# A two-layer trunk on one core: projection weights cast one unit ahead, squares a block later, and a one-product scale

## The chip, the cores and the metric

The kernel runs on one core of a Trainium2 chip. The metric is the device time of one execution in microseconds (us), as the median of several runs. The engines are TensorE (PE: matmuls, with PEld for its weight loads), VectorE (DVE), ScalarE (ACT), GpSimd (POOL) and SyncE (SP, which here issues nearly all DMA transfers). Each engine works through its own instructions in order, and semaphores tie the engines together.

## The reference

A trunk of two pre-norm residual layers over 1024 positions of width 1024, all in float32, and a last norm. The first mixer is a recurrent layer (LRU) of width 1536, the second is attention with 16 heads of 64 and a forget gate (FoX). Cut to what matters:

```python
def lru_mixer(h, ...):
    u = h @ w_in                                   # 1024 -> 2 * 1536
    xb, gate = u[..., :1536], u[..., 1536:]
    xc = causal_depthwise_conv(xb, conv_w, conv_b)
    r, i = sigmoid(block_diag(xc, wa, ba)), sigmoid(block_diag(xc, wx, bx))
    log_a = -8 * r * softplus(-a_param)
    hs = scan(exp(log_a), sqrt(-expm1(2 * log_a)) * i * xc)
    return (hs * silu(gate)) @ w_out

def fox_mixer(h, ...):
    u = h @ w_in                                   # q, k, v, gate, and 16 columns of forget logits
    cum = cumsum(log_sigmoid(f_logit + b_f))
    logits = q @ k.T / 8 + cum[query] - cum[key], masked to key <= query
    return (softmax(logits) @ v * silu(gate)) @ w_out

x = x + lru_mixer(rms_norm(x, g0)); x = x + fox_mixer(rms_norm(x, g1)); out = rms_norm(x, gf)
```

## The kernel before

All work is in one function, `trunk`, written as Python generators that a tile scheduler orders further. Products keep float32 accuracy by splitting each operand into a high and a low part. A product is then three matmuls (high by high, high by low, low by high), and each weight needs two casts: the high part by ACT, and the low part by DVE or POOL.

Four stages follow one another. From about 20 to 440 us run twelve LRU blocks (`for n in range(NB)`). Each loads its weights, casts them (`wh` by ACT, `wl` by POOL or DVE), projects (`ups`, `gps`), and runs convolution, gates and scan on DVE and ACT. Beside this, `some()` lets ACT square a piece of the attention weights (`wsf`), whose norms set the scale with which those weights become float16.

From 440 to about 517 us runs the passage between the layers: the last output products (`ops`), the squares of the new x (`squares`), and then `input_scale(h)` for each half of the sequence. There `xnorm` sums eight columns of squares over all partitions, ACT takes the root (`unit_x`), and DVE forms `gx`, the scale with which `split_input` makes the float16 parts of the layer's input (`h16`). `sscol` are the column sums for the norm itself. The first value products (`vps`) and the first projections of keys and queries (`gps1`) follow.

From 517 to 950 us come the attention heads. A head's work is a string such as `"1.1..1.1..00"`. `run` walks through it: a digit takes a step of the head's own work (1 for scores and maxima, 0 for the weighted sum) and a dot takes one step of the `fill`, which is projection work for later heads, so that PE always has something to do. Scores S go into two PSUM buffers. Each is masked by DVE with its maximum `m`, turned into `p` by an exponential on ACT, normalised to `pp` (ACT the high, DVE the low part), transposed by a DMA (`pT`), and used for O. In heads 3, 7 and 11 the values of the next four heads are projected (`values(g)`, products `vps`).

Projection weights of attention are loaded into raw tiles (`wf`, three buffers) and cast by `split16` into float16 tiles (`w16`, `w` in the profile). `weights16` and `values` call it, and load and casts stand in one place of the program. The scheduler is free to lift them as far as buffers and dependences allow. `tc.issue_after` ties an instruction behind a given one.

From 950 us on come the output projection and the last norm.

The raw tiles come from here:

```python
    return wpool.tile([P, *shape], F32, tag="wf", name="wf", bufs=3)
```

The functions that the change touches:

Of the kernel before, what the change touches and what calls it, by code (L numbers as in the profile page):

```python
# [40 lines left out]
def trunk(ctx: ExitStack, tc: tile.TileContext, xt, w0, wg, wo0, pc, gn, gf, w1, wv, wf, bf, wo1, out):  # L41
# [157 lines left out]
    with ExitStack() as l0:  # L199
# [378 lines left out]
        for h, cs in enumerate(halves):  # L578
# [45 lines left out]
    with ExitStack() as l1:  # L624
# [10 lines left out]
        def fixed_rows():  # L635
            for s in range(2):
                nc.gpsimd.memset(f32(T[s][64:, 1]), 1.0)
                for u in U[s][s:]:
                    nc.vector.memset(f32(u[64:, 1]), 0.0)
                    nc.vector.memset(f32(u[64:68, 1]), -1.0)  # L640

        slots = itertools.cycle(("wh", "wl"))

        def split16(src, shape, b):
# [4 lines left out]
            both = wpool.tile([P, 2, *shape], FP16, tag=next(slots), name="w16")  # L649
# [3 lines left out]
            return [(hi[:, k], lo[:, k]) for k in range(shape[0])]  # L653

        def weights16(b):

            for k in range(0, KT, 4):
                yield from split16([(w1[b][:, k : k + 4], slice(0, P))], (4, P), 4 + b)

        def project(b, w, use, hs=(0, 1)):  # L660

            for h in hs:
                pt = ps.tile([P, HALF], F32, tag="g", name="gps1")
                yield from gemm_steps(pt, zip(w, hT[h]))
                nc.vector.scalar_tensor_tensor(pt, pt, unit_w[:, 4 + b : 5 + b], rs1[h], ALU.mult, ALU.mult)
                use(h, pt)

        def values(g):

            ex = HEADS if g == 0 else 0  # L670
            parts = []
            for k in range(0, KT, 2):
# [12 lines left out]
            for st, k in todo:  # L685
# [18 lines left out]
                for a in range(2):  # L704
                    v = vpool.tile([P, 4, HD], FP16, tag=f"v{st}", name=f"v{st}", bufs=2)
                    src = pt[:, a * P : (a + 1) * P].rearrange("p (b d) -> p b d", b=2)
                    rv_ = rv[:, g, st : st + 1]
                    to_hi(v[:, 0::3], src, nc.scalar, scale=rv_)
                    nc.vector.scalar_tensor_tensor(v[:, 1:3], src, rv_, v[:, 0::3], ALU.mult, ALU.subtract)
                    Vs[2 * g + a].append(v)  # L710
                if ex:
                    nc.vector.tensor_scalar(fz[:, st], pt[:, 256:], rf[:, st : st + 1], None, ALU.mult)
# [10 lines left out]
        def kq_units(pair, parts=((1, (0, 1)), (0, (0, 1)))):  # L723

            for is_k, hs in parts:
                if is_k not in kq:
                    kq[is_k] = tuple(
                        kqpool.tile([P, SEQ], F32R, tag=f"qk{p}{is_k}", name=f"qk{p}") for p in "hl"
                    )
                if hs[0] == 0 or pair == 0 or is_k and pair in (3, 5, 7):  # L730
                    kqw[is_k] = list(weights16(is_k * 8 + pair))
                hi, lo = kq[is_k]

                def use(h, pt):
                    eng = nc.scalar if pair or h else nc.vector
                    cs = halves[h]
                    if is_k:
                        to_hi(hi[:, cs], pt, eng)
                        to_lo(lo[:, cs], pt, hi[:, cs], nc.vector)
                    else:  # L740
                        to_hi(hi[:, cs], pt, eng, scale=0.125)
                        nc.vector.scalar_tensor_tensor(lo[:, cs], pt, 0.125, f32(hi[:, cs]), ALU.mult, ALU.subtract)  # L742

                yield from project(is_k * 8 + pair, kqw[is_k], use, hs)
# [47 lines left out]
        drain(kq_units(0, ((1, (0,)), (0, (0,)))))  # L792
# [53 lines left out]
        def g_units(pair, hs=(0, 1)):  # L846

            if hs[0] == 0:
                sgs[pair] = at.tile([P, SEQ], F32, tag="sg", name="sg1")
                gw[0] = list(weights16(16 + pair))  # L850
            sg = sgs[pair]

            def use(h, pt):
                g_ = sg[:, h * HALF : (h + 1) * HALF]
# [3 lines left out]
            yield from project(16 + pair, gw[0], use, hs)  # L858
# [97 lines left out]
        seen = [None]  # L956

        behind = []

        def run(order, *gens, fill=iter(()), side=iter(()), vals=None):  # L960

            for n, i in enumerate(order):
                if vals and n == order.rfind("1"):
# [185 lines left out]
        fill = kq_units(0, ((1, (1,)), (0, (1,))))  # L1149
# [6 lines left out]
        fill = g_units(0)  # L1156
# [7 lines left out]
        for hd in range(HEADS):  # L1164
            pair = hd // 2
            if hd % 2 == 0:
                if hd < 12:
                    fill = kq_units(pair + 1, ((1, (1,)), (0, (0, 1))))
                    if hd == 0:
                        fill = chain(kq_units(1, ((1, (0,)),)), fill)  # L1170
                elif hd == 12:
# [4 lines left out]
                        kq_units(7, ((1, (1,)), (0, (0, 1)))),  # L1176
                        g_units(7, (0,)),
                        high_y(0),
                        first_out(),
                        beside(g_units(7, (1,)), 1, splits[0]),  # L1180
# [6 lines left out]
            elif pair < 6:  # L1187
                fill = chain(g_units(pair + 1), kq_units(pair + 2, ((1, (0,)),)))
# [4 lines left out]
            run(first, weigh(hd, 0), maxima(hd, 1), fill=fill, side=side)  # L1193
# [10 lines left out]
            vals = None  # L1204
            if hd % 4 == 3 and hd < 12:
                vals = values(hd // 4 + 1)
# [92 lines left out]
```

## Time and profile before

| What | us |
|---|---|
| Median of 3 runs | 1077.0 (1075.47 to 1083.69) |
| Profiled execution | 1077.86 |
| Its span | 1076.1 |
| PE busy | 1036.2 (96% of the span) |
| DVE busy | 789.2 |
| ACT busy | 657.7 |
| POOL busy | 108.8 |
| Mean granted clock of PE | 0.989 |

The span is the time from the first to the last instruction of the profiled execution. PE is the busiest engine by far, and what it waits for is shown in the views of its waits and in the timelines. Lines of a view begin with the start, or with the engine and the line of the program; a bracket at the end gives the idle time before an instruction and what released it. Several groups share one line because helpers issue them: L57 is every ACT instruction of the helper, L69 every matmul, and L66 every load.

### The profile page before, as it was taken

The page shows a single profiled execution, that of the slowest core. Times are in us where ns is not written, and L with a number is a line of the kernel's source. Part 1 is how long each engine was busy: PE and PEld are TensorE (multiplying, and loading weights), DVE is VectorE, ACT ScalarE, POOL GpSimd, SP SyncE. Part 2 cuts the span into 40 slices and gives each one's busy share as a digit, 9 for nine tenths or more (in the row PEclk, how much of TensorE's full clock was granted, in tenths as well). Part 3 has the DMA queues.
Part 4 walks back from the last instruction along what each step waited for, and adds up shares of the span by engine and source line. Part 5 has one row for each costly group of instructions (what it writes and reads, how often), then busy time and mean ns, then how long its engine had stood idle before and what let it go on. Part 6 is the DMA issues. An engine that isn't in the chain of part 4 may idle for free. (4 is left out here: it accounts for less than half of the span.)

```text
span 1076.1 us, 15162 instructions
## 1 busy us (share of the span) xinstructions
PE 1036.2 (96%) x5130; PEld 728.0 (68%) x5130; DVE 789.2 (73%) x1463; ACT 657.7 (61%) x1199; POOL 108.8 (10%) x87
## 2 busy tenths in 40 slices
PE   8998999999999999999899999999999999999997
PEld 6786788788888888766445566544755447577676
DVE  7788686657756868897778876878578884886675
ACT  8468756565657475565666655656466664754454
POOL 1312122022212220001000000000000000012110
PEclk9998999999999999999999999999999999999999
DMA  7112433233323311443678994888848895689984
GB/s 246 60 44 84 118 113 103 84 99 113 102 74 98 122 57 50 148 149 87 164 154 169 180 192 116 154 178 173 177 115 180 168 187 125 129 175 236 257 200 157
DMA packets 219805, 148.92 MB, mean 138 GB/s; under 512 B 161936, under 2 KB 174864, under 8 KB 219728
## 3 DMA queue, kind: packets, MB, share of 16 engines
q1 hardware_dynamic: 217328, 140.09, 54.0%
q0 software_dynamic: 2400, 7.87, 2.4%
q8 instruction: 40, 0.66, 0.3%
q14 instruction: 37, 0.30, 0.1%
HBM read 73.33 MB, written 11.67 MB: 79 GB/s over the span
## 5 line engine op out<-in xcount | busy, mean ns | idle before, releaser
L69 PE MATMUL gps<-h,w 128*128 128x512 f16 x1152 | 272.6, 384 | 2.3 <-DVE qkl L742 2.3
L69 PEld LDWEIGHTS <-w 128*128 128x128 f16 x1152 | 104.8, 99 | 130.2 <-issue 19.8
L57 ACT ACTIVATE p<-S,m 128x128 f32<-128x128 f32 (+7 forms) x128 | 94.2, 736 | 61.8 <-DVE m L889 37.5
L69 PE MATMUL S<-T,U 96*128 96x512 f32 (+7 forms) x384 | 106.3, 386 | 17.9 <-ACT p L57 17.8
L110 POOL TENSOR_TENSOR wl<-wf,wh 128x512 fp32r<-128x512 f32 x46 | 87.5, 1910 | 315.8 <-ACT wh L57 203.1
L57 ACT ACTIVATE pp<-p,sums 128x128 f16<-128x128 f32 (+7 forms) x128 | 95.5, 770 | 33.2 <-DVE sums L901 12.4
L903 DVE SCALAR_TENSOR_TENSOR pp<-p,sums,pp 128x128 f16<-128x128 f32 (+7 forms) x128 | 102.8, 813 | 13.1 <-ACT pp L57 12.2
L889 DVE CUSTOM_DVE_ANT_0 S<-S,mask 128x128 f32<-128x128 f32 (+7 forms) x128 | 97.1, 759 | 11.1 <-PE S L69 10.1
L69 PEld LDWEIGHTS S<-T,U 128*128 128x128 f32 (+1 forms) x384 | 67.2, 190 | 43.6 <-ACT p L57 29.5
L69 PE MATMUL vps<-w,h 128*128 128x256 f16 (+1 forms) x768 | 88.4, 277 | 0.5 <-ACT v L57 0.5
L57 ACT CAST wh<-wf 128x512 fp32r<-128x512 f32 x88 | 51.5, 592 | 56.6 <-PE ops L69 31.2
L69 PEld LDWEIGHTS <-h 128*128 128x128 f16 x768 | 75.8, 99 | 12.2 <-ACT v L57 0.8
L69 PE MATMUL gps<-hh,wl 128*128 128x512 f32 x192 | 76.8, 400 | 4.6 <-POOL wl L110 4.5
L69 PE MATMUL ops<-yh,wh 128*128 128x512 f32 x192 | 77.4, 403 | 0.7 <-DVE x L403 0.7
L69 PE MATMUL ups<-hh,wh 128*128 128x512 f32 x192 | 76.2, 398 | 1.4 <-ACT hh L57 1.3
L69 PE MATMUL ops<-yh,wl 128*128 128x512 f32 x192 | 76.3, 397 | 0.7 <-DVE wl L110 0.7
L69 PE MATMUL ups<-hl,wh 128*128 128x512 f32 x192 | 76.3, 397 | 0.2
L69 PE MATMUL ups<-hh,wl 128*128 128x512 f32 x192 | 75.7, 394 | 0.8 <-POOL wl L110 0.8
L69 PE MATMUL gps<-hl,wh 128*128 128x512 f32 x192 | 76.4, 398 | 0.0
L69 PE MATMUL gps<-hh,wh 128*128 128x512 f32 x192 | 76.4, 398 | 0.0
L69 PE MATMUL ops<-yl,wh 128*128 128x512 f32 x192 | 75.6, 400 | 0.0
L57 ACT ACTIVATE w<-wf,wsq 128x512 f16<-128x512 f32 (+1 forms) x74 | 52.4, 717 | 37.8 <-PE gps L69 14.2
(197 smaller groups left out, 1910.7 us busy)
## 6 DMA issues: line engine op xcount, KB each, us to landing
wf<-in_w SPq DMA_DIRECT2D x106, 256.0 KB
wsf<-in_w SPq DMA_DIRECT2D x48, 256.0 KB
wf<-in_wo SPq DMA_DIRECT2D x64, 128.0 KB
T<-qkh SPq DMA_DIRECT2D x64, 128.0 KB
U<-qkh SPq DMA_DIRECT2D x64, 128.0 KB
x<-in_xt SPq DMA_DIRECT2D x16, 256.0 KB
wsf<-in_wv SPq DMA_DIRECT2D x16, 256.0 KB
x1d<-x SPq DMA_DIRECT2D x16, 256.0 KB
```

The source lines that it names most:

```text
L57: act[0] = op(*args, **kw)
L69: pe[0] = nc.tensor.matmul(*args, **kw)
L110: return eng.tensor_tensor(lo, src, f32(hi), ALU.subtract)
L889: nc.vector.tensor_tensor_reduce(S[:, :n], S[:, :n], mask[:, SEQ - n :], -1.0, -NEG, ALU.add, ALU.min, accum_out=m)
L903: nc.vector.scalar_tensor_tensor(both[:, :, 1], p, r, both[:, :, 0], ALU.mult, ALU.subtract)
```

## The change

Five things are changed.

The squares of the attention weights begin in block 3 of the LRU and no longer in block 2; `some()` is called once more in each block.

In the passage, `xnorm` is one product of eight columns for each half. ACT copies its result into `gx` and sums the eight columns on the way (`accum_out`), and takes the root from that sum. The last square of the first half is added up like the others by DVE, without the flag `wait`.

The rows of U that hold constants are written by ACT copies of `onesf` with a scale of 0 or -1, not by DVE memsets.

Weights of projections are objects (`Weights`) with a load and a cast of their own. `play` walks through the units of a plan. In the last half of a unit it loads the next unit's weights at step 0, and casts them at step 2, tied behind `seen[0]`, which is the last exponential. All fills are planned ahead in the list `fills`.

`values` loads its first two weights in the first run of the head (`soon`), and casts them before the second run; the last two are loaded and cast in the second run.

```diff
         def some():
-            if n > 1:
+            if n > 2:
                 with tc.issue_after(act[0].ins):
                     next(wsquares, None)
...
             product(ups[1], 1, wu)
+            some()
...
             nc.vector.tensor_tensor(xsq[h], xsq[h], g2, ALU.mult)
-            all_ = ps.tile([P, 1], F32, tag="O", name="xnorm")
-            for k in range(KT):
-                matmul(all_, onesf, xsq[h][:, k : k + 1], start=k == 0, stop=k == KT - 1)
-            nc.scalar.activation(unit_x[h], all_, AF.Sqrt, bias=tiny, scale=1.0 / TOP / TOP)
+            all_ = ps.tile([P, KT], F32, tag="O", name="xnorm")
+            matmul(all_, onesf, xsq[h], start=True, stop=True)
+            nc.scalar.activation(gx[h], all_, AF.Copy, accum_out=unit_x[h])
+            nc.scalar.activation(unit_x[h], unit_x[h], AF.Sqrt, bias=tiny, scale=1.0 / TOP / TOP)
...
-                        wait=h == 0 and db == KT - 1,
                         accum=xsq[h][:, db : db + 1],
...
                 for u in U[s][s:]:
-                    nc.vector.memset(f32(u[64:, 1]), 0.0)
-                    nc.vector.memset(f32(u[64:68, 1]), -1.0)
+                    for rows, value in ((slice(64, P), 0.0), (slice(64, 68), -1.0)):
+                        one = onesf[rows, :1]
+                        nc.scalar.activation(
+                            u[rows, 1], one.to_broadcast([one.shape[0], HALF]), AF.Copy, scale=value
+                        )
...
+        class Weights:
+            def load(self):
+                if self.raw is None:
+                    self.raw = [
+                        load16([(w1[self.b][:, k : k + 4], slice(0, P))], (4, P), 4 + self.b) for k in range(0, KT, 4)
+                    ]
+            def cast(self):
+                self.load()
+                if self.parts is None:
+                    self.parts = [x for r in self.raw for x in cast16(*r)]
+                return self.parts
...
+        def play(units):
+            for u in units:
+                u["start"]()
+                w, h = u["w"], u["h"]
+                after_ = [v["w"] for v in plan[plan.index(u) + 1 :] if v["w"] is not w][:1]
                 pt = ps.tile([P, HALF], F32, tag="g", name="gps1")
+                for i, _ in enumerate(gemm_steps(pt, zip(w.cast(), hT[h]))):
+                    if h == u["last"] and seen[0] is not None:
+                        for v in after_:
+                            if i == 0:
+                                v.load()
+                            elif i == 2:
+                                with tc.issue_after(seen[0].ins):
+                                    v.cast()
+                    yield
...
         def values(g):
-            parts = []
+            parts, raw = [], []
             for k in range(0, KT, 2):
...
-                parts += split16(src, (2, 256 + ex), g)
-                if k == 2 or k == 6 and not ex:
+                raw.append(load16(src, (2, 256 + ex), g))
+                if k == 2 and not ex:
+                    yield
+                if k % 4 == 0:
+                    continue
+                with tc.issue_after(seen[0].ins) if k == 2 and not ex else nullcontext():
+                    parts += [x for r in raw for x in cast16(*r)]
+                raw = []
+                if k == 2 or not ex:
                     yield
...
             for n, i in enumerate(order):
+                if soon and n == order.rfind("1") + 1:
+                    next(soon)
                 if vals and n == order.rfind("1"):
                     next(vals)
```

How this moves instructions stands at three places. The first is ACT in head 3, from the end of one run of scores into the next. `w16` from `wf_5389` is the second value weight; `wf_5401` and `wf_5403`, and in the rows of before `wf_5854` and `wf_5940`, are weights of projection units. Before:

```order
L57 ACTIVATE yo_5160<-O_5418,wsq_238 64x512
L57 ACTIVATE p_5447,sums_5440<-S_5442,m_5445 128x128
L57 ACTIVATE w16_5856<-wf_5854,wsq_238 128x512
L57 ACTIVATE p_5468,sums_5440<-S_5463,m_5466 128x256
L57 ACTIVATE sg1_5313<-gps1_5405 128x512
L57 ACTIVATE w16_5942<-wf_5940,wsq_238 128x512
```

And with the change:

```order
L57 ACTIVATE yo_5145<-O_5411,wsq_238 64x512
L57 ACTIVATE w16_5426<-wf_5389,wsq_238 128x512
L57 ACTIVATE p_5436,sums_5429<-S_5431,m_5434 128x128
L57 ACTIVATE w16_5450<-wf_5401,wsq_238 128x512
L57 ACTIVATE w16_5453<-wf_5403,wsq_238 128x512
L57 ACTIVATE p_5463,sums_5429<-S_5458,m_5461 128x256
L57 ACTIVATE sg1_5308<-gps1_5394 128x512
```

The cast that stood behind the first exponential (128x128) now stands ahead of it, and two more casts stand ahead of the second one.

The second place is SP in the same head, with the change: the transfers around the last value load, `wf_5510`.

```order
L66 DMA wf_5502<-in_w1 128x512
L66 DMA wf_5504<-in_w1 128x512
L66 DMA wf_5508<-in_wv 128x512
L967 DMA_TRANSPOSE pT_5430<-pp_5438 128x2x128
L967 DMA_TRANSPOSE pT_5430<-pp_5465 128x4x128
L66 DMA T1_3806<-cumd_3798 2x512
L967 DMA_TRANSPOSE pT_5430<-pp_5486 128x6x128
L66 DMA T1_3806<-qkh_3822 64x512
L66 DMA wf_5510<-in_wv 128x512
```

Three raw loads go out together and fill the three buffers. The fourth comes six transfers later, when the cast of `wf_5508` has given its buffer back.

The third place is ACT in the LRU around block 2, where `wh` is the weight whose low part POOL makes. Before:

```order
L57 CAST xch_629<-xc_623 128x1024
L57 ACTIVATE wsf_596,vsq_237<-wsf_596 128x256 x2
L57 ACTIVATE ti_570<-gate_586,hbx_111 128x512
L57 CAST yh_591<-a_522 128x1024
L57 ACT_TABLE_LOAD
L57 ACTIVATE m2_719<-m2_719 128x1024
L57 CAST wh_900<-wf_898 128x512
```

And with the change:

```order
L57 CAST xch_627<-xc_621 128x1024
L57 ACTIVATE ti_570<-gate_586,hbx_111 128x512
L57 CAST yh_591<-a_522 128x1024
L57 ACT_TABLE_LOAD
L57 ACTIVATE m2_703<-m2_703 128x1024
L57 CAST wh_876<-wf_874 128x512
```

The pair of squares `wsf_596` ahead of the cast `wh` is gone from this block. The order of PE is the same in both kernels from the first scores of attention to the end.

More of the change, by code (lines that the diff above doesn't have):

```diff
@@ L848, in g_units, with start @@
             if hs[0] == 0:
-                sgs[pair] = at.tile([P, SEQ], F32, tag="sg", name="sg1")
-                gw[0] = list(weights16(16 + pair))
-            sg = sgs[pair]
+                gw[0] = Weights(16 + pair)
+            def start():
+                if pair not in sgs:
+                    sgs[pair] = at.tile([P, SEQ], F32, tag="sg", name="sg1")
             def use(h, pt):
-                g_ = sg[:, h * HALF : (h + 1) * HALF]
+                g_ = sgs[pair][:, h * HALF : (h + 1) * HALF]
                 nc.scalar.activation(g_, pt, AF.Tanh, scale=0.5)
                 nc.vector.scalar_tensor_tensor(g_, g_, 1.0, pt, ALU.add, ALU.mult)
-            yield from project(16 + pair, gw[0], use, hs)
+            units = [job(gw[0], h, start, use) for h in hs]
+            for u in units:
+                u["last"] = hs[-1]
+            return units
         stats, pT = {}, {}
@@ L1148, in late @@
                 late_w.append((wh, wl))
-        fill = kq_units(0, ((1, (1,)), (0, (1,))))
+        fills = [kq_units(0, ((1, (1,)), (0, (1,)))), g_units(0), []]
+        for pair in range(7):
+            if pair == 0:
+                fills[-1] += kq_units(1, ((1, (0,)),))
+            fills[-1] += kq_units(pair + 1, ((1, (1,)), (0, (0, 1))))
+            if pair < 6:
+                fills += [g_units(pair + 1) + kq_units(pair + 2, ((1, (0,)),)), []]
+        last_g = [g_units(7, (h,)) for h in range(2)]
+        fills = iter(fills)
+        fill = play(next(fills))
         gates1 = forget(1)
@@ L1155, in trunk @@
         drain(fill)
-        fill = g_units(0)
+        fill = play(next(fills))
         for _ in range(4):
@@ L1167, in trunk @@
                 if hd < 12:
-                    fill = kq_units(pair + 1, ((1, (1,)), (0, (0, 1))))
-                    if hd == 0:
-                        fill = chain(kq_units(1, ((1, (0,)),)), fill)
+                    fill = play(next(fills))
                 elif hd == 12:
@@ L1187, in trunk @@
             elif pair < 6:
-                fill = chain(g_units(pair + 1), kq_units(pair + 2, ((1, (0,)),)))
+                fill = play(next(fills))
             first, second = LAST if hd > 11 else ORDER
@@ L1192, in trunk @@
             side = chain(pieces(hd + 1, 0, 0), pieces(hd + 1, 0, 1)) if hd else iter(())
-            run(first, weigh(hd, 0), maxima(hd, 1), fill=fill, side=side)
+            vals = values(hd // 4 + 1) if hd % 4 == 3 and hd < 12 else None
+            run(first, weigh(hd, 0), maxima(hd, 1), fill=fill, side=side, soon=vals)
             drain(side)
@@ L1203, in trunk @@
                 side = chain(side, late())
-            vals = None
-            if hd % 4 == 3 and hd < 12:
-                vals = values(hd // 4 + 1)
+            if vals:
                 next(vals)
```

88 lines of the change are left out of this document (50 added, 38 removed).

## The prediction

> **What bounds the kernel now.** I read four views in this order: the engines' busy time, the list of what TensorE (PE) waits for, the timelines around its longest waits, and the granted clock by stretch.
>
> ```profile
> PE 1036.2 (96%) x5130; PEld 728.0 (68%) x5130; DVE 789.2 (73%) x1463; ACT 657.7 (61%) x1199; POOL 108.8 (10%) x87
> PE S L69 <- ACT p L57: 17.8, 19, 2.0
> PE gps L69 <- POOL wl L110: 4.5, 1, 4.5
> PE gps L69 <- DVE qkl L742: 2.3, 1, 2.3
> ```
>
> The first row is each engine's busy time, the others are PE's waits: total, count, longest. PE is busy for 1036.2 of the span's 1076.1 us, so about 40 us are to be had from waits. The rest must come from fewer matmul passes or from a better clock. Of the waits, 17.8 us stand before score products (S), whose PSUM buffer is freed by an exponential (p) on ScalarE (ACT). The timeline names what holds the exponential back:
>
> ```profile
> 659.47 0.72 ACT L57 ACTIVATE w<-wf,wsq 128x512 f16<-128x512 f32 x1 [1.84 <-DMA wf<-in_w]
> 660.10 0.78 ACT L57 ACTIVATE p<-S,m 128x640 f32<-128x640 f32 x1
> 661.01 0.98 PE L69 MATMUL S<-T,U 128*128 128x512 f32 x4 [2.02 <-ACT p L57]
> 702.67 0.74 PE L69 MATMUL S<-T,U 128*128 128x512 f32 x2 [2.00 <-ACT p L57]
> 788.50 1.01 PE L69 MATMUL S<-T,U 128*128 128x512 f32 x4 [2.03 <-ACT p L57]
> ```
>
> The columns are start, duration, engine and operation, with the idle time before it in brackets. At 659.47 a weight cast waits 1.84 us for its own DMA. The exponential behind it starts at 660.10, and PE goes on at 661.01 after 2.02 us.
>
> ```profile
> 88.00:100.00 12.00, 7.54 (x22) 5.67 (x22) 10.90 (x9) 11.16 (x25) 5.68 (x1) 0.72 0.37 117
> 440.00:460.00 20.00, 19.21 (x93) 14.91 (x92) 16.73 (x31) 12.59 (x29) 0.00 (x0) 0.91 0.43 147
> 470.00:490.00 20.00, 20.00 (x140) 14.59 (x137) 18.54 (x40) 12.02 (x24) 2.18 (x3) 0.91 0.39 119
> 655.00:665.00 10.00, 7.99 (x49) 5.17 (x47) 7.29 (x18) 6.94 (x14) 0.00 (x0) 1.00 0.33 107
> 784.00:794.00 10.00, 7.97 (x34) 4.10 (x32) 6.89 (x17) 6.21 (x12) 0.00 (x0) 0.83 0.46 134
> ```
>
> These rows give a stretch, its length, the busy time of PE, PEld, DVE, ACT and POOL, the granted clock, the DMA share and GB/s. The loss to the clock is length times (1 - clock): 12 x 0.28 = 3.4, twice 20 x 0.09 = 1.8, nothing, and 10 x 0.17 = 1.7 us. The first and last of these stand around waits of 4.46 and 2.03 us. At 440 and 470 PE hardly idles; around the wait of 661.01 the clock is whole.
>
> By the Trainium skill (TensorE: Matmul & The Clock Gate, Part 1: The HAM clock gate) the clock falls to half after an idle window of about 3.4 us. The rows for 440, 470 and 784 disagree: the clock fell there with no wait over 2.03 us. By that rule alone the change would not win the clock terms below, and the sum would be 3.5 us higher.
>
> **Part 1, the scale product in the passage.** Two groups of one-column products stand in the path of PE:
>
> ```profile
> 450.87 1.84 PE L69 MATMUL xnorm<-xsq,onesf 128*128 128x1 f32 x16
> 452.57 1.93 PE L69 MATMUL sscol<-onesf,sq 128*128 128x1 f32 x16
> 475.76 1.92 PE L69 MATMUL xnorm<-xsq,onesf 128*128 128x1 f32 x16
> 477.54 1.03 PE L69 MATMUL sscol<-onesf,sq 128*128 128x1 f32 x8
> ```
>
> Sixteen passes fill 450.87 to 452.57, or 1.70 us. Over all four rows 56 passes take 6.2 us, 0.11 each. The change makes each xnorm one product of eight columns (two passes each), which removes 28 passes. Summing the last square of the first half on VectorE (DVE) removes 8 more sscol passes. That is 36 x 0.11 = **-4.0 us**. The eight-column product is not in the trace; I price it like a one-column pass. Both low-clock stretches of the passage begin right behind these rows. With 1.1 us of such passes in place of 3.5 and 2.7 the clock may hold: **-2.5**, between 0 and -3.6. Against this, the first half's scale now stands behind an added copy with a sum and behind squares of the second half on ACT, and PE takes up the first projection earlier. A wait of 0 to 3 us can appear: **+1**.
>
> **Part 2, squares a block later.** The LRU's longest wait, under the row of its group (busy time, then the mean of one in ns):
>
> ```profile
> L110 POOL TENSOR_TENSOR wl<-wf,wh 128x512 fp32r<-128x512 f32 x46 | 87.5, 1910 | 315.8 <-ACT wh L57 203.1
> 83.13 0.43 ACT L57 ACTIVATE wsf<-wsf 128x256 f32<-128x256 f32 x1
> 83.85 0.20 ACT L57 ACTIVATION_READ_ACCUMULATOR wsf<-wsf 128x1 f32 x1
> 86.86 1.22 DVE L311 TENSOR_TENSOR us<-ups,rs 128x1024 f32<-128x1024 f32 x1
> 87.84 1.13 ACT L57 CAST wh<-wf 128x512 fp32r<-128x512 f32 x2
> 88.00 1.21 DVE L110 TENSOR_TENSOR yl<-a,yh 128x1024 fp32r<-128x1024 f32 x1
> 88.52 5.68 POOL L110 TENSOR_TENSOR wl<-wf,wh 128x512 fp32r<-128x512 f32 x1 [14.64 <-ACT wh L57]
> 94.26 0.79 PE L69 MATMUL gps<-hh,wl 128*128 128x512 f32 x1 [4.46 <-POOL wl L110]
> ```
>
> The POOL subtraction takes 5.68 us beside a run of DVE operations, and PE waits 4.46 for it. The change removes the squares that stood ahead of the cast wh: some 0.8 us from 83.13 on. It also puts yl ahead of us on DVE, so that POOL's operation meets a DVE operation that reads PSUM. If POOL then takes 1.9 us, the mean of its group, the wait and its 3.4 us of clock go, together -7.9. If only the start moves, -0.8. The later blocks get the squares instead, which could cost 1. I take **-3.5**, a little under half of the best case.
>
> **Part 3, start of attention.** Late casts there end in waits of PE:
>
> ```profile
> 488.33 1.57 DVE L639 MEMSET U<- 64x512 f32 x3 [0.16 <-DVE v L709]
> 507.13 0.72 ACT L57 ACTIVATE w<-wf,wsq 128x512 f16<-128x512 f32 x1 [2.30 <-DMA wf<-in_w]
> 509.33 1.33 ACT L57 ACTIVATE w<-wf,wsq 128x512 f16<-128x512 f32 x2 [1.22 <-DMA wf<-in_w]
> 521.05 1.46 PE L69 MATMUL gps<-h,w 128*128 128x512 f16 x6 [2.32 <-DVE qkl L742]
> 523.75 0.62 PE L69 MATMUL S<-T,U 128*128 128x384 f32 x2 [1.24 <-ACT p L57]
> ```
>
> The change loads these weights a unit earlier, so 3.5 us of ACT waits leave the chain to qkl. Of PE's 2.32 + 1.24 I take **-2.5**, between 0 and -3.6. U's constants move from DVE (three of the six memsets take 1.57 us) to six ACT copies, some 0.7 us each if they run like the casts above. The vps products of that place cover both, so they cost nothing, and up to 1 us if a v eviction slips.
>
> **Part 4, weights one unit ahead.** The weights cast at 659 and 786 are now loaded some 20 us before their use by the order of the units, so the waits of 2.02 and 2.03 go, with perhaps half of the 1.7 us of clock at 786: **-5**, between 0 and -5.8. The wait at 702.67 stays, since the order there is as before. Moving casts off DVE near 600, 727 and 853 should save about 0.7 each, the 0.74 us of the DVE cast at 594.39 below: **-2**, between 0 and -2. Two or three unit weights keep only 2.3 to 3.7 us between issue and use, where the two loads in the rows below take 2.8 and 3.8 from issue to the cast's start: **+1.5**, between 0 and +3.
>
> Against this stand the **values stages** (heads 3, 7 and 11). Before, their weights were cast during earlier heads. Now all four casts, and four unit casts, come within about 20 us. The same place in the trace, with the two rows just used on top:
>
> ```profile
> 594.39 0.74 DVE L652 SCALAR_TENSOR_TENSOR w<-wf,wsq,w 128x512 f16<-128x512 f32 x1
> 656.70 1.25 SPq L66 DMA_DIRECT2D wf<-in_w  x2
> 623.62 1.55 SPq L66 DMA_DIRECT2D wf<-in_w  x3
> 625.40 0.37 ACT L57 ACTIVATE p<-S,m 128x128 f32<-128x128 f32 x1
> 627.46 0.72 ACT L57 ACTIVATE w<-wf,wsq 128x512 f16<-128x512 f32 x1 [1.60 <-DMA wf<-in_w]
> 625.91 0.62 PE L69 MATMUL S<-T,U 128*128 128x384 f32 x2 [0.19 <-ACT p L57]
> 628.69 0.73 PE L69 MATMUL S<-T,U 128*128 128x512 f32 x2 [0.84 <-ACT p L57]
> 635.97 9.22 PE L69 MATMUL vps<-w,h 128*128 128x256 f16 x83
> 635.67 1.24 ACT L57 ACTIVATE pp<-p,sums 128x384 f16<-128x384 f32 x2
> ```
>
> First wait: the load issued at 623.62 lands at 627.46, after 3.8 us. Before, the exponential at 625.40 stood ahead of its cast. Now a value cast stands ahead of that exponential. It can start only at 627.46 + 0.63 = 628.1, and with two more casts of 0.72 before the second exponential the next S slips from 628.69 to about 631.5: **+2.8**. If the load lands as the cast comes up, 0.
>
> Second wait: raw weights have three buffers, and the last value load now waits for the cast before last. That cast follows the two normalisations (pp) that end at 636.91 in the last row, later by up to the 2.8 just found; its two halves take 1.4, so it ends between 638.3 and 641.1, say 639.8. A load of 2.8 to 3.8 us and the last cast's own 1.4 make the last weight ready at 644.0 to 645.0. PE, at 0.11 us per vps, needs it 30 products into the stage: 635.97 + 2.8 + 3.3 = 642.1. That is a wait of 1.9 to 2.9; the other ends of the cast give 0.4 and 4.2. I take **+1.9**, since SP has less queued there. Behind these casts on ACT stand the evictions v, and behind those the value products' PSUM.
>
> Together 4.7 in each of three stages, **+14**; between 0 and 3 x (2.8 + 4.2 + 1.7) = 26, the last term for a drop of the clock as at 784.
>
> By the Trainium skill (DMA: Bandwidth & Descriptors, two cost components) a transfer costs about 2.0 us plus its bytes at 436 GB/s, which for these 256 KB is 2.6 us. The row at 623.62 shows 3.8, with other transfers in flight. With the page's 2.6 the first wait would be 1.2 us shorter and the second 0.2, and the sum by it some 4 us lower, towards the faster case below.
>
> **The sum.** -4.0 - 2.5 + 1 - 3.5 - 2.5 - 5 - 2 + 1.5 + 14 = -3.0 us. The profiled execution took 1077.86 us (span 1076.1 and 1.8 around it), 0.9 above the median of 1077.0. So 1077.86 - 3.0 = **1074.9 us**.
>
> **The rivals.**
>
> *Faster, 1062 us.* The loads land before their casts come up in the values stages. For it: SP then has fewer issues ahead of them, and the load at 656.70 took 2.8 us. Against it: the third-buffer chain is fixed by the allocation. The stages then cost 1 us each, not 4.7 (-11), and part 2 wins 2 more: 1074.9 - 13 = 1062.
>
> *Slower, 1090 us.* In each values stage the waits come at 2.8 and 2.9 us and the clock falls behind them, as behind 2.03 us at 784: 7.4 each, 22 in all, +8 against my sum. The wait in the passage takes its 3 (+2), and parts 2 and 3 and the passage's clock win only 3 of 8.5 (+5.5): 1074.9 + 15.5 = 1090. For it speaks that the first wait is tied to one load's place; against it, that at 659 a wait of 2.02 us left the clock whole. It decides from about 6.8 us per stage: the other terms are -17 as I take them and -9.5 if these fail, and 1% is 10.8.
>
> *It does little, 1078 us.* PE's order from the first S on is the one of before, and each wait may only move to the next exponential. Then the passage's 4 us stay and the stages take them back. This lies within the same 1% as my forecast.
>
> **How the numbers follow.** I give my forecast 0.28 and doing little 0.14, together 0.42 within 1% (1066 to 1088); 1% is about what a measurement of this kernel can tell from no change. The faster case has 0.34, since most terms are gains read from single waits and only one term is a large loss. The slower case has 0.24. With all gains whole and no loss the sum is about -27 us (1051), and with all losses and only the 4.0 of the passage won +30 (1108). The range for 8 in 10 leaves a tenth at either end: 1056 to 1092. The forecast's own range is 1066 to 1082.
>
> **What would show it.** Right: PE's wait on POOL wl falls below 2 us, xnorm shows 4 passes, and no S waits 2 us in the places of 659 and 786. Right for the loss: in heads 3, 7 and 11 a value cast on ACT waits for its DMA with an exponential behind it, and PE's vps wait on DVE w or ACT w, about 4 us per stage. Wrong: vps runs without a break in these stages (then it is the faster case), or the clock's low stretches become more than before (the slower one).

## The result and the profile after

The changed kernel takes 1086.2 us (median of 14 runs, 1083.6 to 1092.4), the kernel before 1077.5 in its runs beside it. The ratio is 1.0073 with a 95% interval of 1.0053 to 1.0093: **slower by 0.7%**, where the forecast was 1074.9. The profiled execution took 1086.31 us with a span of 1084.5.

PE's waits in the changed kernel (total, count, longest):

```profile
PE S L69 <- ACT p L57: 11.9, 6, 4.2
PE gps L69 <- DVE w L661: 9.8, 8, 2.0
PE vps L69 <- ACT v L57: 7.8, 1, 7.8
PE gps L69 <- ACT w L57: 1.9, 1, 1.9
```

The wait on POOL's wl of 4.5 us and the one on qkl of 2.3 are gone, and the waits before S fell from 17.8 us in 19 to 11.9 in 6. But the longest of them are now over 4 us, and two kinds are new: 11.7 us of projections (gps) that wait for a weight cast (w), and 7.8 us of value products (vps) that wait for an eviction.

Where the time went is seen from the first exponential of the heads, before and after:

```profile
523.24 0.36 ACT L57 ACTIVATE p<-S,m 128x128 f32<-128x128 f32 x1
```

```profile
514.33 0.36 ACT L57 ACTIVATE p<-S,m 128x128 f32<-128x128 f32 x1
```

The first exponential comes 8.9 us earlier, and the last matmul ends 8.4 us later. Of the 8.9 us, 5.3 are there at the first score product (512.65 against 517.91); the rest are the waits of 2.32 and 1.24 us at the start of attention, which are gone. So the stages up to here win 8.9 us in these two executions, and attention from here on loses 17.3.

**What won.** In LRU block 2, POOL's subtraction and the DVE operation beside it (after), and the clock there:

```profile
87.36 1.51 POOL L110 TENSOR_TENSOR wl<-wf,wh 128x512 fp32r<-128x512 f32 x1 [13.85 <-ACT wh L57]
87.63 1.21 DVE L311 TENSOR_TENSOR us<-ups,rs 128x1024 f32<-128x1024 f32 x1
88.00:100.00 12.00, 11.45 (x51) 9.01 (x49) 11.78 (x11) 10.28 (x15) 0.86 (x1) 1.00 0.25 71
```

POOL's subtraction starts 1.16 us earlier, lies for most of its time beside the operation that reads PSUM, and takes 1.51 us where it took 5.68. PE does not wait, and the granted clock of the stretch is 1.00 where it was 0.72. In the passage xnorm is down to four passes (count, then minimum, median and maximum in ns), and the low clock around it is gone:

```profile
L69 PE MATMUL xnorm<-xsq,onesf x4: 170/214/256, 444.3 to 466.4; 128*128 128x8 f32 x4
440.00:460.00 20.00, 19.96 (x93) 13.15 (x93) 19.13 (x40) 16.28 (x39) 0.00 (x0) 1.00 0.55 175
```

**What lost.** First, still ahead of attention, a new wait at the passage's end:

```profile
470.98 5.00 ACT L57 ACTIVATE h<-x,gx 128x512 f16<-128x512 f32 x8
478.32 1.66 ACT L57 ACTIVATE U<-onesf 64x512 fp32r<-64x512 f32 x3 [1.88 <-DVE h L573]
480.01 0.88 ACT L57 ACTIVATE v<-vps,rv 128x128 f16<-128x128 f32 x3
484.01 1.52 PE L69 MATMUL vps<-w,h 128*128 128x272 f16 x6 [7.83 <-ACT v L57]
476.00:488.00 12.00, 4.17 (x26) 2.86 (x25) 5.97 (x17) 7.81 (x17) 4.28 (x5) 0.72 0.44 99
```

PE began the value products 16 us earlier than before. It ran through what PSUM holds, and then waited for evictions that stand on ACT behind the second half's split (h) and U's copies. The granted clock of this stretch is 0.72.

Second, a unit weight whose cast is tied behind an exponential, in head 5:

```profile
664.79 1.01 SPq L66 DMA_DIRECT2D wf<-in_w  x2
697.23 0.37 ACT L57 ACTIVATE p<-S,m 128x128 f32<-128x128 f32 x1
697.59 0.71 ACT L57 ACTIVATE w<-wf,wsq 128x512 f16<-128x512 f32 x1
699.99 0.74 DVE L661 SCALAR_TENSOR_TENSOR w<-wf,wsq,w 128x512 f16<-128x512 f32 x1
700.79 1.43 PE L69 MATMUL gps<-h,w 128*128 128x512 f16 x5 [2.03 <-DVE w L661]
```

The second of the two loads at 664.79 (matched by the order of instructions) brings the weight that is cast at 697.59, some 32 us later and right behind the exponential. PE needs it at 698.4 and waits 2.03 us, until its low part, which DVE takes up at 699.99 behind other work, is done. Four more places show the same.

Third, the value stage of head 3:

```profile
617.89 0.59 SPq L66 DMA_DIRECT2D wf<-in_wv  x1
622.29 0.72 ACT L57 ACTIVATE w<-wf,wsq 128x512 f16<-128x512 f32 x1 [2.63 <-DMA wf<-in_wv]
622.92 0.35 ACT L57 ACTIVATE p<-S,m 128x128 f32<-128x128 f32 x1
623.41 1.01 PE L69 MATMUL S<-T,U 128*128 128x384 f32 x2 [3.40 <-ACT p L57]
```

The load takes 4.4 us to the cast, the exponential waits behind the cast, and PE waits 3.40. In heads 7 and 11 the same wait is 2.75 and 4.19 us. The clock falls behind these waits and behind some of those for unit weights:

```profile
520.00:530.00 10.00, 7.68 (x30) 4.00 (x30) 6.79 (x18) 7.74 (x14) 0.00 (x0) 0.83 0.79 170
620.00:632.00 12.00, 7.73 (x24) 3.31 (x24) 8.43 (x23) 6.08 (x16) 0.00 (x0) 0.72 0.91 218
698.00:706.00 8.00, 5.97 (x21) 2.55 (x20) 6.99 (x21) 4.39 (x12) 0.00 (x0) 0.79 1.01 214
752.00:762.00 10.00, 7.13 (x24) 3.11 (x25) 8.03 (x22) 5.98 (x15) 0.00 (x0) 0.83 0.99 240
828.00:836.00 8.00, 5.97 (x21) 2.41 (x21) 6.52 (x20) 4.76 (x12) 0.00 (x0) 0.79 0.98 201
880.00:892.00 12.00, 6.94 (x23) 3.10 (x23) 8.28 (x23) 5.98 (x15) 0.00 (x0) 0.72 1.01 233
```

By length times (1 - clock), which is an estimate, these cost 1.7, 3.4, 1.7, 1.7, 1.7 and 3.4 us, 13.6 in all. The kernel before has two such stretches in attention, the one at 784 and this one, each 1.7 us:

```profile
698.00:708.00 10.00, 7.84 (x28) 3.04 (x27) 6.87 (x17) 4.57 (x13) 0.00 (x0) 0.83 0.95 212
```

So some 10 of the 17.3 us are clock, and the wait of 2.03 us in head 5 stands in place of the one of 2.00 us before S at 702.67.

### The profile page after: what moved, and what is told of

Read it like the earlier page. It is cut to its first block, busy times and chain, and to the rows that moved or that the text cites. A ratio compares the mean times of both kernels' runs of the same rounds, so it can differ in the third digit from the quotient of the medians.

```text
span 1084.5 us, 15083 instructions
## 1 busy us (share of the span) xinstructions
PE 1035.9 (96%) x5094; PEld 724.5 (67%) x5094; DVE 786.8 (73%) x1456; ACT 660.3 (61%) x1211; POOL 95.8 (9%) x87
## 5 line engine op out<-in xcount | busy, mean ns | idle before, releaser
L69 PE MATMUL gps<-h,w 128*128 128x512 f16 x1152 | 278.9, 389 | 11.8 <-DVE w L661 9.8
L69 PE MATMUL S<-T,U 96*128 96x512 f32 (+7 forms) x384 | 110.6, 398 | 12.2 <-ACT p L57 11.9
L110 POOL TENSOR_TENSOR wl<-wf,wh 128x512 fp32r<-128x512 f32 x46 | 74.5, 1623 | 320.4 <-ACT wh L57 267.0
L69 PEld LDWEIGHTS S<-T,U 128*128 128x128 f32 (+1 forms) x384 | 69.8, 195 | 35.2 <-ACT p L57 18.4
L403 DVE TENSOR_TENSOR x<-x,ops 128x512 f32<-128x512 f32 x80 | 54.2, 681 | 27.5 <-PE ops L69 27.2
```

Source lines behind the costliest of these rows:

```text
L69: pe[0] = nc.tensor.matmul(*args, **kw)
L110: return eng.tensor_tensor(lo, src, f32(hi), ALU.subtract)
L403: nc.vector.tensor_tensor(x, x, pt, ALU.add)
```

## The experiments

My theory on seeing the two traces was A: the time is lost at two stretches, behind U's copies in the passage and behind the value casts of heads 3, 7 and 11. The rival was B: the forced places of the unit casts lose it.

Each ratio is against the kernel before on the same chip, with its 95% interval. Edits 1 to 6, 10, 11, 13 and 14 are made to the changed kernel, 7, 8, 9 and 12 to the kernel before. The changed kernel also holds two small edits that the list of five leaves out: the evictions of the first value products have a higher priority, with the forget column (fz) ahead of them (the order of evictions below), and the high part of the first keys and queries is written by ACT and not by DVE.

**1. U's constants by DVE again.**

```diff
-                    for rows, value in ((slice(64, P), 0.0), (slice(64, 68), -1.0)):
...
+                    nc.vector.memset(f32(u[64:, 1]), 0.0)
+                    nc.vector.memset(f32(u[64:68, 1]), -1.0)
```

> The changed kernel with U's constants set by DVE memsets again; nothing else is touched. Theory A (two stretches lose the time: ACT behind U's copies in the passage, and ACT behind the value casts of heads 3, 7 and 11): the wait of 7.83 us before vps falls below 2 us and the low clock behind it goes, so 1077 to 1080 us instead of 1086. Theory B (the forced places of the unit casts lose the time, the passage does not matter since PE only reaches the next wait earlier): within 2 us of 1086.

Measured 1086.7 us, ratio 1.0109 (1.0087 to 1.0132): nothing is won. The wait of PE stays, with another name, and the rows behind it show why:

```profile
472.78 4.72 DVE L573 SCALAR_TENSOR_TENSOR h<-x,gx,h 128x512 f16<-128x512 f32 x7
477.59 0.66 DVE L752 TENSOR_SCALAR fz<-vps,rf 128x16 f32<-128x16 f32 x4
477.86 1.14 ACT L57 ACTIVATE v<-vps,rv 128x128 f16<-128x128 f32 x4 [2.08 <-DVE fz L752]
483.63 1.52 PE L69 MATMUL vps<-w,h 128*128 128x272 f16 x6 [8.11 <-DVE v L758]
```

The evictions wait for fz on DVE, which stands behind the split of the second half. U's copies were only the last of what stood there, so the first half of theory A falls.

**2. Value weights as before, unit weights forced.**

```diff
-                raw.append(load16(src, (2, 256 + ex), g))
...
+                parts += split16(src, (2, 256 + ex), g)
+                if k == 2 or k == 6 and not ex:
                     yield
...
-            run(first, weigh(hd, 0), maxima(hd, 1), fill=fill, side=side, soon=vals)
+            run(first, weigh(hd, 0), maxima(hd, 1), fill=fill, side=side)
```

> The changed kernel with the value weights loaded and cast where the kernel before did it: both in one step and free for the scheduler to lift. Theory A: the waits before S of 3.40, 2.75 and 4.19 us go, and the low clock of five windows behind them (1.7 us each); 10 us of waits and 8 of clock less some new ones: 1068 to 1075 us. Theory B: the waits for unit weights stay and take most of it: 1081 us or more.

Measured 1095.4 us, 1.0188 (1.0165 to 1.0210): slower than the changed kernel. It lies in theory B's open range, but neither theory forecast that the split helps while the unit weights have forced places. The waits before S did shrink, to 4.0 us in 5. PE waited for casts of weights on ACT in their place: 11.4 us in 4 before projections (gps) and 8.4 us in 6 before value products (vps). Theory A's second half as it stood falls too.

**3. Unit weights free, all else as changed.**

```diff
-                    if h == u["last"] and seen[0] is not None:
+                    if False:
```

> The changed kernel without the forced loads and casts of unit weights: each unit's weights are loaded and cast at the unit's own start and the scheduler may lift them; the plan and all else stay. Theory A: PE's waits for w (11.7 us in 9) are replaced by the waits of the kernel before of S behind casts, so 1082 to 1089 us. Theory B: these waits go with their low clock: 1072 to 1077 us.

Measured 1076.3 us, 0.9995 (0.9980 to 1.0011): the forced unit weights cost 0.8%, as theory B said. PE's waits for w are gone:

```profile
PE S L69 <- ACT p L57: 22.1, 15, 3.9
PE vps L69 <- ACT v L57: 7.8, 1, 7.8
PE O L69 <- DMA pT<-pp: 2.3, 2, 1.7
```

**4. Unit weights, value weights and U as before** (the three edits above together).

> The changed kernel with U's constants, value weights and unit weights as before, so that only the squares and the scale of the passage are changed. Theory A: entry into attention is some 9 to 13 us earlier than before and attention costs what it cost before: 1064 to 1069 us. Theory B's wider form (attention is bound by its own chain of casts and gives an earlier start back): 1073 to 1078 us.

Measured 1073.4 us, 0.9983 (0.9967 to 1.0000): in the range of theory B's wider form. But its trace does not show that attention gives the early start back: the first exponential is 6.7 us earlier than before, and the last matmul still 5.9.

**5. The tie of unit casts taken away.**

```diff
-                                with tc.issue_after(seen[0].ins):
-                                    v.cast()
+                                v.cast()
```

> The changed kernel, but the casts of unit weights are not tied behind the last exponential: loads at step 0 and casts at step 2 of the unit before keep their places in the program, and the scheduler may lift the casts. Theory B1 (the tie holds back casts of weights that landed 25 to 50 us earlier): PE's waits for w of units fall from 11.7 to below 3 us and three low-clock windows go: 1073 to 1078 us. Theory B2 (the place of the loads is what is late, or the raw buffers): the waits stay: 1083 us or more.

Measured 1083.4 us, 1.0074 (1.0051 to 1.0097): no gain, so B1 falls. The time is the one of B2, but not its mechanism, since the waits for unit weights did go. Others took their place:

```profile
PE S L69 <- ACT p L57: 18.5, 16, 2.6
PE vps L69 <- DVE v L760: 7.3, 3, 3.2
```

**6. Both ties taken away.**

```diff
-                with tc.issue_after(seen[0].ins) if k == 2 and not ex else nullcontext():
+                with nullcontext():
```

> As the run without the tie of unit casts, and the tie of the first value casts is taken away as well. If the value tie costs what the S waits of 3.40, 2.75 and 4.19 us show, 5 to 10 us less than with that tie: 1066 to 1072 us. If those waits come from the late value load and not from the tie, within 2 us of the run without the unit tie.

Measured 1078.9 us, 1.0038 (1.0022 to 1.0055), 4.5 us below run 5 and so between the two forecasts. The value tie costs, but the waits before S in the stages stay (3.23, 2.93 and 4.45 us). In head 3:

```profile
615.53 0.60 SPq L66 DMA_DIRECT2D wf<-in_wv  x1
619.31 0.72 ACT L57 ACTIVATE w<-wf,wsq 128x512 f16<-128x512 f32 x1 [2.45 <-DMA wf<-in_wv]
619.94 0.35 ACT L57 ACTIVATE p<-S,m 128x128 f32<-128x128 f32 x1
```

Without any tie a value cast still stands ahead of the first exponential and waits for its load.

**7. The squares alone.**

```diff
-            if n > 1:
+            if n > 2:
...
             product(ups[1], 1, wu)
+            some()
```

> The kernel before with the squares a block later and one more step of them in each block; nothing else. Theory: the LRU ends 6 to 7 us earlier (the POOL wait at block 2 and its low clock) and nothing gives it back: 1069 to 1072 us. Rival: the passage's chain on ACT gives it back: 1074 to 1077 us.

Measured 1068.9 us, 0.9942 (0.9920 to 0.9963): as the theory said, **a gain of 6 us**. POOL's wl takes 1.50 us here as well. This version beats both kernels.

**8. The passage alone.**

```diff
...
-            for k in range(KT):
-                matmul(all_, onesf, xsq[h][:, k : k + 1], start=k == 0, stop=k == KT - 1)
...
+            matmul(all_, onesf, xsq[h], start=True, stop=True)
+            nc.scalar.activation(gx[h], all_, AF.Copy, accum_out=unit_x[h])
...
-                        wait=h == 0 and db == KT - 1,
```

> The kernel before with the one-product scale and without the waiting flag of the last square; nothing else. Theory: 4 us of PE passes and 1 to 3 of the clock are saved up to attention, and PE waits for value evictions at its end for what it gained: 1073 to 1076 us. Rival (PE's work in the passage is the path): 1070 to 1072 us.

Measured 1076.0 us, 1.0004 (0.9990 to 1.0019): worth nothing. PE now waits for evictions at the end of the passage:

```profile
486.41 0.85 PE L69 MATMUL vps<-w,h 128*128 128x272 f16 x6 [3.76 <-DVE fz L711]
```

**9. Squares and passage** (edits 7 and 8 together).

> The kernel before with the squares and the passage of the change; attention's program is the one of before. Theory: the passage alone was worth nothing and the squares 6 us, so together 1067 to 1071 us. Rival: the passage's 4 us are lost here as in the run with all of attention's parts undone, which stood some 4 us above the squares alone: 1071 to 1075 us.

Measured 1072.1 us, 0.9956 (0.9936 to 0.9975). The time lies in the rival's range, but the kernel before took 1077.0 us on this chip and 1074.8 on that of run 7. By the ratios (0.9942 for the squares alone) the intervals overlap: the squares' gain, nothing from the passage, and no loss that can be told from it.

**10. Unit weights loaded a half earlier, casts still tied.**

```diff
-                    if h == u["last"] and seen[0] is not None:
+                    if seen[0] is not None:
...
-                            elif i == 2:
+                            elif i == 2 and h == u["last"]:
```

> The changed kernel with the next unit's weights loaded at step 0 of every half and so a half earlier where a unit has two; the tied casts stay at their place. Theory B2 (the loads' place makes the value stages crowd): 1078 to 1083 us. Theory B3 (raw buffers are held by casts that come late, so an earlier load holds them longer): 1086 us or more.

Measured 1091.0 us, 1.0131 (1.0104 to 1.0158): an earlier load makes it slower, as B3 forecast. No row here shows that the raw buffers are the reason. PE's waits for w grow:

```profile
PE gps L69 <- ACT w L57: 11.5, 4, 4.2
PE gps L69 <- DVE w L661: 10.5, 8, 2.0
PE vps L69 <- ACT w L57: 5.8, 5, 2.6
```

**11. Half of the value weights left out.**

```diff
+                if k > 2 and not ex:
+                    if k == 6:
+                        parts += parts[:4]
+                        yield
+                    continue
```

> The changed kernel with the last two of four value weights of heads 3, 7 and 11 not loaded and not cast (the products take the first two again, so the values differ). This takes six loads and six casts out of the three crowded stages. Theory B3 (four unit and four value weights share three raw buffers within a stage): each stage loses 2 to 3 us less: 1077 to 1081 us. Theory A (only the first tied value cast ahead of the exponentials costs): within 2 us of 1086.

Measured 1081.4 us, 1.0041 (1.0023 to 1.0059): by the ratio 3 to 4 us less, just outside B3's range. The waits of 3.36, 3.86 and 3.56 us before S stay, so the crowd in the stage is only part of the loss.

**12. Squares, and U's constants by ACT** (edit 7, and edit 1 the other way round).

```diff
-                    nc.vector.memset(f32(u[64:, 1]), 0.0)
-                    nc.vector.memset(f32(u[64:68, 1]), -1.0)
+                    for rows, value in ((slice(64, P), 0.0), (slice(64, 68), -1.0)):
...
```

> The kernel before with the squares a block later and U's constants by ACT; nothing else. Theory: U's constants are neutral: within 2 us of the squares alone, 1068 to 1071 us. Rival: ACT's copies wait behind DVE's split of the input and hold the value evictions: 1072 us or more.

Measured 1071.1 us, 0.9938 (0.9913 to 0.9964): U's constants are neutral.

**13. Unit weights free and no value tie** (edits 3 and 6).

> The changed kernel without the forced loads and casts of unit weights, and without the tie of the first value casts; loads and casts of values keep their split places in the program. Theory B4 (a tied cast keeps raw buffers that others need, so every tie costs): faster than with the value tie (0.9995 of the kernel before), 0.996 to 0.999, or 1073 to 1076 us at a before of 1077. Rival (with free unit casts the value tie costs nothing, the loads' place in the second run does): 0.999 to 1.002.

Measured 1069.5 us, 0.9960 (0.9945 to 0.9976), as B4 forecast: against run 3 the value tie costs 0.35%, and 0.36% between runs 5 and 6. That every tie costs does not hold, since the unit tie costs nothing (run 5), and that held raw buffers are the reason is not shown. In head 3 the waiting cast, here of a unit weight, stands behind the exponential again:

```profile
617.76 0.37 ACT L57 ACTIVATE p<-S,m 128x128 f32<-128x128 f32 x1
619.78 0.72 ACT L57 ACTIVATE w<-wf,wsq 128x512 f16<-128x512 f32 x1 [1.56 <-DMA wf<-in_w]
```

**14. Unit weights and value weights as before** (edits 2 and 3).

> The changed kernel with unit and value weights as before; squares, passage, U by ACT and the order of the evictions stay as changed. If U by ACT and the eviction order cost nothing: as squares and passage alone, 0.994 to 0.997 of the kernel before. If the forget column ahead of the value evictions costs what the passage's wait of 7.8 us shows over the 3.5 of squares and passage alone: 0.998 to 1.001.

Measured 1069.8 us, 0.9964 (0.9949 to 0.9978): with run 13, splitting the value loads costs nothing as long as the unit weights are free and nothing is tied, and U's copies and the order of evictions cost nothing that shows here. This run has the passage's wait of 7.8 us, run 9 has one of 3.5, and they take the same time. Run 4 lies higher by 0.2% than this, with U by DVE; the intervals overlap, and I did not find out whether it is more than noise.

**The sum.** Squares, passage, U and eviction order: 0.9964 (run 14), and 0.9960 with the value loads split (run 13). From run 13 single edits lead to the changed kernel: forced unit loads and casts, untied, +0.0078 (run 6); the value tie, +0.0036 (run 5); the unit tie, 0. Such a chain must end at the 1.0073 that was measured, so its end bears nothing out. What does is that runs 13, 6, 3 and 5 are the four combinations of two edits: the forced unit weights cost 0.78% without the value tie (run 6 against 13) and 0.79% with it (run 5 against 3). The parts do not add up everywhere: the split of the value loads costs nothing in run 13, and without it run 2 is 1.1% slower than the changed kernel.

Two things can be measured behind this. The lead of a cast is the time from the end of the low cast to PE's first use of the weight, matched by the order of instructions, over the last 60 weights; below 0, PE's first product, which needs only the high part, ran before the low part was done. The loss in the value stages is by how much PE falls back against the kernel before, from a score product ahead of a stage (the 91st, 181st and 281st of the 384) to the stage's last value product, summed over heads 3, 7 and 11. In the changed kernel PE is 5.7 us ahead before head 3's stage and 1.3 us behind after it, which makes 7.0 for this stage.

| Kernel | median lead, us | shortest | weights that PE waits for | loss in the value stages, us |
|---|---|---|---|---|
| before | 36.8 | 20.9 | 0 | |
| changed | 3.9 | -2.4 | 11 | 18.9 |
| run 10, loads a half earlier | 2.9 | -2.4 | 16 | 26.1 |
| run 3, units free | 25.9 | 4.6 | 0 | 11.3 |
| run 5, no unit tie | 25.1 | -0.7 | 2 | 17.0 |
| run 6, no ties | 40.2 | 14.6 | 0 | 14.6 |
| run 13, units free, no tie | 36.9 | 20.9 | 0 | 0.4 |

"One unit ahead" is later than before. The scheduler had cast these weights some 37 us ahead, in gaps of ACT and DVE. This is where PE's new waits for w come from, but it is not the 0.8%: runs 5 and 6 have long leads again, run 5 is as slow as the changed kernel, and run 6 still lies 0.8% above run 13. The loss is in the value stages, and the times by and large follow it: 27.0 us in run 2, the slowest, and 1.9 in run 14. In the changed kernel and in runs 3 and 6, a value cast that waits for its load stands ahead of the first exponential in all three stages; in run 13 in none, as the rows of runs 6 and 13 show for head 3. In runs 2 and 10 the waiting cast stands behind that exponential in head 3, and PE waits for the unit weight instead. That these waits and their low clock are all of the loss is my reading of the traces. Run 6 is 0.9 us ahead of run 13 before head 3's stage and 12.5 behind after head 11's, more in these two executions than the 8 us by the ratios.

## Why the prediction was wrong

By PE's place in the two executions, parts 1 to 3 brought -8.9 us up to the first exponential (forecast: -11.5), the value stages +18.9 (forecast: +14), and the rest of attention, where the unit weights were to win, about -1.5 (forecast: -5.5).

- **Part 1, the passage, -4.0 - 2.5 + 1.** The passes and the two low-clock stretches went as predicted, though the clock fell anew behind the wait at the end (12 x 0.28 = 3.4 us by the row for 476, about what the two stretches had cost). But PE's work was not the path there: run 8 is worth nothing. The step that failed is the wait, bounded by 0 to 3 us and taken as 1. It was 7.8 us in the changed kernel and 3.8 in run 8. I looked for it in front of the first projections, and it came at the value products. Evictions queue behind the split of the second half, and PE, being early, meets them.
- **Part 2, the squares, -3.5.** The mechanism was right and the term too small: some 6 us in runs 7 and 12, within the bounds to -7.9. POOL took 1.51 us, below the 1.9 of the best case.
- **Part 3, start of attention, -2.5.** The waits of 2.32 and 1.24 went, 3.6 us in all. Soon after, PE waited 1.87 and 0.45 us for a tied unit cast at 522 (the first of the five places), and the clock fell behind it (1.7 us by the row for 520), so that nothing was left.
- **Part 4, unit weights, -5 - 2 + 1.5.** This is the step that turned the sign. By the runs forcing these weights costs 0.8%, some 8 us, where I had -5.5. I looked at the two waits of a cast for its load at 659 and 786, which did go, and took a fixed place as the cure. But those casts were not late: the weight cast at 659 is first used at 705 (matched by the order of instructions), and the median lead was 36.8 us. The forced casts ended within a few us of their use, and PE's 11.7 us of waits for them are more than what those two waits had cost. The larger error is that I added the unit weights and the value stages as separate terms. They share ACT and the raw buffers there: the loss in the stages is 18.9 us with forced unit weights and 11.3 without (run 3), and without the value tie 14.6 and 0.4 (runs 6 and 13).
- **Part 4, value stages, +14.** The first wait was found where it was predicted: a value cast ahead of the first exponential of heads 3, 7 and 11, 3.40, 2.75 and 4.19 us against 2.8. The second was smaller, 0.4 to 1.2 us against 1.9. The clock fell behind each, which I kept for the upper bound only; those rows give 3.4, 1.7 and 3.4 us. So the stages cost about 24 us in waits and clock, with 0.9 in each for a tied unit cast, near the 26 that bounded them, or 18.9 against the kernel before, which had waits of its own there. The term was too small, by its clock above all. Run 13 bears the mechanism out: with that cast behind the exponential again it is 7.7 us ahead of the kernel before ahead of head 3's stage, and 8.8 after head 11's.
- **The clock.** By the Trainium skill's rule (TensorE: Matmul & The Clock Gate, Part 1: The HAM clock gate) the clock falls to half after an idle window of some 3.4 us. This trace disagrees again: the clock fell behind the waits of 2.03 and 2.75 us (rows for 698 and 752). My own sign for the slower case, more low stretches than before, came true.
- **The load.** By the other page of the Trainium skill (DMA: Bandwidth & Descriptors, two cost components) the value load would take about 2.6 us, an estimate from its figures, which it gives for transfers that GpSimd issues. This load was issued by SyncE. It took 4.4 us from its issue at 617.89 to the start of the cast that waited for it at 622.29, and the measurement decides.
- **The rivals.** The slower one, with its stages at 7.4 us each, was nearest in mechanism. Its passage wait and its falling clock both came, but not its loss of the squares' gain. It kept my -5.5 for the unit weights, so that its 1090 lies near the measured 1086.2 is partly luck.

## What to carry to other kernels

Before loads and casts are tied to places, measure for each weight the time from the end of its cast to its first use. Where a scheduler already has tens of microseconds of lead, as here, the waits have another cause, and a forced "one ahead" can be a step back. By the traces the cause was a cast that waited for its load ahead of the work that frees the next PSUM buffer, so look at what stands behind such a cast. Weights that share an engine and buffers are one term and not two. And test each edit alone: here the squares alone (0.9942) beat the whole change by 1.3%.

## What the runs showed of the hardware

The same subtraction on POOL took 5.68 us when it started 0.5 us into a DVE operation with both operands in SBUF (yl, at 88.00), with others of that kind behind it. It took 1.51 us when it started 0.3 us before the end of such an operation and then lay beside one that reads PSUM (us, from 87.63 to 88.84). And a wait of 3.40 us cost PE as much again through the clock (3.4 us by the row for 620), where one of 2.03 us cost 1.7 (the row for 698). Both prices of the clock are estimates by length times (1 - clock).
